# The modulation's products on VectorE instead of TensorE, in a two-block transformer kernel

## The chip, the cores and the metric

The kernel runs on one core of a Trainium2 chip. The metric is the device time of one execution in microseconds (us); the median of a few executions is quoted. A core has five engines with their own queues of instructions: PE (TensorE, matrix products), DVE (VectorE), ACT (ScalarE), POOL (GpSimd) and SP (SyncE, which here only starts DMA transfers). Each engine takes its instructions in order, and waits for the others through semaphores.

## What is computed

One batch of 256 tokens of 1024 features goes through two layers of a first block (three mixing branches, a gated feed-forward and a per-layer gate) and then through two layers of a second block, which also carries 256 context tokens. All tensors are float32. The second block modulates its normalized input by numbers that come from two vectors, `c` and `c_ctx`, through a matrix of 1024 x 6144 for each layer:

```
s_lat, s_ctx = silu(c), silu(c_ctx)[None, :]
for i in range(DEPTH):                                   # DEPTH = 2
    sh1, sc1, g1, sh2, sc2, g2 = split(s_lat @ ada_w[i] + ada_b[i], 6)
    a_l = rms_norm(h_lat, norm_g[i, 0]) * (1 + sc1) + sh1
    if ctx_in:                                           # both layers
        csh1, csc1, cg1, csh2, csc2, cg2 = split(s_ctx @ ada_w[i] + ada_b[i], 6)
        a_c = rms_norm(h_ctx, norm_g[i, 0]) * (1 + csc1) + csh1
    ...                                                  # pooling (i = 0) or attention (i = 1)
    h_lat = h_lat + g1 * y_l
    h_lat = h_lat + g2 * sq_relu_mlp(rms_norm(h_lat, norm_g[i, 1]) * (1 + sc2) + sh2)
    if ctx_out:                                          # only i = 0
        h_ctx = ...                                      # the same with the csh, csc and cg
```

So layer 0 needs all 6144 modulation numbers for both vectors, and layer 1 needs all of them for `c` but only the first 2048 (`csh1`, `csc1`) for `c_ctx`. These products are vector times matrix: 2 x 1024 x 6144 weights are read once each and used for at most two multiplications.

## The kernel before

**Tiling.** Activations lie with a feature to a partition: `x` is 128 partitions x 8 feature blocks x 256 tokens. Every weight is cut on the host into blocks of 128 x 128, and eight blocks make a chunk of 128 x 1024 (512 KB). `_plan` (L264) lists all 610 chunks in the order in which the program consumes them: 514 chunks of ordinary weights (`u`, `ug`, `kr`, ... `m211`) and 96 of the modulation's matrix (`ada0` and `ada1`, 48 each). The function `add` in it drops an ada chunk behind an ordinary one whenever the running sum `due` of the `share` arguments reaches 1, so `share=0.5` means one ada chunk behind every second ordinary chunk.

**The stream.** `Stream` (L310) loads ordinary chunks into four `raw` buffers by DMAs from SP, and ada chunks into two buffers of their own (`ADA_BUFS`). An ordinary chunk is then split in two float32r tiles: ACT rounds it to `hi` (L372), and DVE makes `lo = raw - hi` (L381). There are five `hi` and five `lo` buffers, so casts run at most four chunks ahead of the product in progress. `mm3` (L565) forms each product of a block by three matmuls, `hi` by the high part of the activation (L567), `hi` by its low part (L568) and `lo` by its high part (L569).

**The loop.** `linear` (L616) walks through the blocks of one weight. At each chunk's start it calls `st.get`, which writes the pending `lo` subtractions, the next casts and the next loads, and `bg_step`, which advances background work (norms, splits, softmax pieces, the context's pooling). Where a PSUM bank is complete it calls the evacuation. At each chunk's end `chunk_end` (L611) looks whether the plan has an ada chunk next, and if so calls `ada_chunk` (L592). The order in which the program is written is the order on every engine (`manual_schedule`, L434).

**The modulation before.** `ada_chunk` multiplies on PE: four matmuls (L602) of 128 rows x 256 columns, with `c` and `c_ctx` (after Silu, in the zero-padded tile `s32`) as two of 32 stationary columns, each into its own group of 32 partitions. Sixteen chunks, which are eight pieces of 256 features in two halves of the input, share one PSUM bank. Then ACT copies the bank out (L608), and `ada_turn` (L577) transposes it with two PE transposes (L584), sums the four groups on DVE (L587) and adds the bias `adab` (L590). There are six such turns. `mod_cols` (L1289) later makes `1 + scale` times the norm's gain. It runs for layer 0 inside the background work `ctx_pool` (L1396, during the second `ff`), and for layer 1 right behind `m101` (L1535).

**Names of the stages**, in the order of the plan: `u ug kr fq fk fv ga gc uq uk uv brc bra gb brb wo ff dn pl pg`, once for each layer of the first block (a digit 0 or 1 behind the name), the attentions running inside `ga` to `brb`; then `m100`, `m200`, `m101`, `m201` (the second block's first layer, the first two once for the context and once for `x`, `m101` on both at once), `k v q awo m110 m111 m210 m211`. In the kernel before, `ada0` is consumed from `ff0` to `fk1` and `ada1` from `ff1` to the second `m200`.

Of the kernel before, what the change touches and what calls it, by code (L numbers as in the profile page):

```python
# [30 lines left out]
AG = 8  # L31
# [64 lines left out]
def _weights(I):  # L96
# [6 lines left out]
    for i in range(DEPTH):  # L103
# [53 lines left out]
def _param_cols():  # L157
# [22 lines left out]
def _params(I):  # L180
# [238 lines left out]
def body(ctx: ExitStack, tc: tile.TileContext, dram, outT):  # L419
# [153 lines left out]
    s32 = cp.tile([P, 8, 2 * AG + 30], F32, name="s32")  # L573
    ada_r = cp.tile([P, 2, P], F32, name="ada_r")
    ada_at = {}

    def ada_turn():  # L577

        if "done" not in ada_at:
            return  # L580
        i, c = ada_at.pop("done")
        pt = sc_p.tile([P, 512], F32, tag="sc", name="pt_ada")
        for e in range(2):
            T.transpose(pt[:, e * P:(e + 1) * P], ada_r[:, e], ident)  # L584
        for e in range(2):
            o = ada[:, i, :, c + e:c + 2 * AG:2]
            V.reduce_sum(out=o.rearrange("p c q -> p q c"), axis=AX.X,  # L587
                         in_=pt[:, e * P:(e + 1) * P].rearrange("p (g q c) -> p q c g", g=4, c=2)[:, 0:AG])
        o = ada[:, i, :, c:c + 2 * AG]
        V.tensor_tensor(out=o, in0=o, in1=pc(f"adab{i}", c, c + 2 * AG)[:, None, :].to_broadcast([P, 2, 2 * AG]), op=ALU.add)  # L590

    def ada_chunk():  # L592

        name, c, _ = plan[st.pos]
# [2 lines left out]
        q, half = c // 2 % AG, c % 2
        if q == half == 0:
            ada_at["bank"] = sc_p.tile([P, 512], F32, tag="sc", name="ps_ada")
        ps = ada_at["bank"]  # L600
# [1241 lines left out]
```

## Time and profile before

| what | value |
| --- | --- |
| median of three executions | 1687.11 us (1686.91 to 1689.14) |
| the profiled execution | 1686.17 us, of which the span of the profile is 1684.4 us |
| PE busy | 1663.3 us (99%) |
| DVE busy | 1148.6 us (68%) |
| ACT busy | 889.4 us (53%) |
| POOL busy | 127.5 us (8%) |
| bytes moved | 329.76 MB, mean 196 GB/s |
| granted PE clock | mean 0.998 of full speed |

The span is the time between the first and the last instruction of the profile; 1.8 us of the execution lie around it, and the median stands 0.9 us above the profiled execution. PE's busy time counts overlapping matmuls once, so a PE at 99% says that it almost never waits, not that each product is at its fastest. Durations of DVE instructions include a short tail in which the next instruction may already run, so two neighbours can overlap by about 0.08 us.

### The profile page before, as it was taken

The numbers are of one execution on the slowest core, as the hardware profiler recorded it, in microseconds if no ns is written. First come the engines' busy times: TensorE is split into PE (matmuls) and PEld (weight loads), VectorE is DVE, ScalarE is ACT, GpSimd is POOL, SyncE is SP. The second block draws the span as 40 slices with busy tenths as digits, with TensorE's granted clock in tenths as the row PEclk, the third lists the DMA queues.
The fourth block names the chain that finished last, engine by engine and source line by source line (L and its number), as shares of the span: only waits on it lengthen the run. The fifth ranks groups of instructions, "written<-read, shape, count | busy, mean of one in ns | idle before, by whom it ended". The sixth has DMA issues, their size and how long they took to land.

```text
span 1684.4 us, 33981 instructions
## 1 busy us (share of the span) xinstructions
PE 1663.3 (99%) x14106; PEld 1582.2 (94%) x14106; DVE 1148.6 (68%) x1757; ACT 889.4 (53%) x1329; POOL 127.5 (8%) x128
## 2 busy tenths in 40 slices
PE   8999999999999999999999999999999999999998
PEld 7999998999989899999999999999999999899998
DVE  7888876564577788776886569664446666766654
ACT  6665564443455565655555455553334565667633
POOL 6100100000020000011000000100000011010001
PEclk9999999999999999999999999999999999999999
DMA  7546557777676465577767666666326554145553
GB/s 260 172 148 189 173 172 260 249 252 252 241 244 238 164 176 176 163 257 236 227 214 261 222 218 239 232 218 212 113 89 190 189 178 130 52 161 188 188 189 100
DMA packets 91738, 329.76 MB, mean 196 GB/s; under 512 B 10400, under 2 KB 11072, under 8 KB 91456
## 3 DMA queue, kind: packets, MB, share of 16 engines
q1 hardware_dynamic: 89712, 322.19, 57.6%
q10 hardware_dynamic: 1296, 4.33, 0.8%
q8 instruction: 110, 1.80, 0.4%
q0 software_dynamic: 576, 1.08, 0.3%
q14 instruction: 44, 0.36, 0.1%
HBM read 325.43 MB, written 1.05 MB: 194 GB/s over the span
## 4 chain that ended last, share of the span: by engine, by line
PE 92%; issue 3%; DVE 2%; POOL 1%; ACT 0%; DMA 0%; SPq 0%; POOLq 0%; DVEq 0%; ACTq 0%
PE ps_mm L567 27%; PE ps_mm L568 26%; PE ps_mm L569 26%; PE ps_ada L602 3%; PE sc L781 1%; PE ps_o L822 1%; POOL cols L714 1%; DVE lo L381 1%; PE ps_go L1693 1%; PE ps_w L1080 1%; PE ps_w L1081 1%; PE ps_w L1079 1%; PE ps_l L849 0%; PE sc L782 0%; PE ps_gt L1687 0%
## 5 line engine op out<-in xcount | busy, mean ns | idle before, releaser
L372 ACT ACTIVATE hi<-raw 128x1024 fp32r<-128x1024 f32 x513 | 537.8, 1057 | 386.2 <-PE ps_mm L568 291.4
L381 DVE TENSOR_TENSOR lo<-raw,hi 128x1024 fp32r<-128x1024 f32 x513 | 620.9, 1228 | 96.5 <-ACT hi L372 94.0
L567 PE MATMUL ps_mm<-S1h_t,hi 128*128 128x256 f32 (+1 forms) x1456 | 413.5, 284 | 0.0
L568 PE MATMUL ps_mm<-S1l_t,hi 128*128 128x256 f32 (+1 forms) x1456 | 405.7, 279 | 0.0
L569 PE MATMUL ps_mm<-S1h_t,lo 128*128 128x256 f32 (+1 forms) x1456 | 405.3, 278 | 0.0
L567 PE MATMUL ps_mm<-S0h_t,hi 128*128 128x256 f32 x1200 | 339.6, 283 | 6.3 <-ACT hi L362 6.3
L569 PE MATMUL ps_mm<-S0h_t,lo 128*128 128x256 f32 x1200 | 333.9, 278 | 0.2 <-DVE lo L381 0.2
L568 PE MATMUL ps_mm<-S0l_t,hi 128*128 128x256 f32 x1200 | 333.9, 278 | 0.1
L567 PEld LDWEIGHTS ps_mm<-S1h_t,hi 128*128 128x128 f32 x1456 | 274.5, 189 | 17.1 <-issue 15.5
L568 PEld LDWEIGHTS ps_mm<-S1l_t,hi 128*128 128x128 f32 x1456 | 274.1, 188 | 0.3
L569 PEld LDWEIGHTS ps_mm<-S1h_t,lo 128*128 128x128 f32 x1456 | 274.3, 188 | 0.0
L567 PEld LDWEIGHTS ps_mm<-S0h_t,hi 128*128 128x128 f32 x1200 | 226.9, 189 | 15.3 <-issue 7.3
L569 PEld LDWEIGHTS ps_mm<-S0h_t,lo 128*128 128x128 f32 x1200 | 226.2, 188 | 0.6 <-DVE lo L381 0.4
L568 PEld LDWEIGHTS ps_mm<-S0l_t,hi 128*128 128x128 f32 x1200 | 226.3, 189 | 0.4 <-DVE S0l_t L751 0.3
L692 POOL TENSOR_TENSOR acc<-acc,sq 128x512 f32<-128x512 f32 x24 | 34.4, 1435 | 817.8 <-ACT sq L684 817.7
L567 PE MATMUL ps_mm<-K_t,hi 128*128 128x256 f32 x320 | 89.6, 280 | 0.0
L568 PE MATMUL ps_mm<-GG_t,hi 128*128 128x256 f32 x320 | 88.5, 276 | 0.0
L569 PE MATMUL ps_mm<-K_t,lo 128*128 128x256 f32 x320 | 88.4, 276 | 0.0
L567 PE MATMUL ps_mm<-VV_t,hi 128*128 128x256 f32 x288 | 80.5, 279 | 0.0
L569 PE MATMUL ps_mm<-VV_t,lo 128*128 128x256 f32 x288 | 79.6, 276 | 0.0
L1493 DVE TENSOR_TENSOR P_t<-P_t 128x512 f32<-128x512 f32 x32 | 21.4, 690 | 77.5 <-ACT P_t L1492 77.5
L568 PE MATMUL ps_mm<-GX_t,hi 128*128 128x256 f32 x256 | 70.9, 277 | 0.0
(434 smaller groups left out, 3070.1 us busy)
## 6 DMA issues: line engine op xcount, KB each, us to landing
raw<-in_w_m_dram SPq DMA_DIRECT2D x176, 512.0 KB, 4.3
raw<-in_w_ada_dram SPq DMA_DIRECT2D x96, 512.0 KB, 4.4
raw<-in_w_ff_dram SPq DMA_DIRECT2D x88, 512.0 KB, 4.5
raw<-in_w_dn_dram SPq DMA_DIRECT2D x44, 512.0 KB, 4.6
raw<-in_w_ga_dram SPq DMA_DIRECT2D x16, 512.0 KB, 4.1
raw<-in_w_gc_dram SPq DMA_DIRECT2D x16, 512.0 KB, 3.6
raw<-in_w_gb_dram SPq DMA_DIRECT2D x16, 512.0 KB, 4.2
raw<-in_w_wo_dram SPq DMA_DIRECT2D x16, 512.0 KB, 3.6
```

The costliest lines, as they stand in the source:

```text
L372: self.nc.scalar.activation(out=h[:, :n], in_=raw[:, :n], func=AF.Copy)
L381: self.nc.vector.tensor_tensor(out=l[:, :n], in0=raw[:, :n], in1=h[:, :n].bitcast(F32), op=ALU.subtract)
L567: T.matmul(ps, lhsT=wh, rhs=ah, start=first, stop=False, skip_group_check=free)
L568: T.matmul(ps, lhsT=wh, rhs=al, start=False, stop=False, skip_group_check=free)
L569: T.matmul(ps, lhsT=wl, rhs=ah, start=False, stop=last, skip_group_check=free)
L602: T.matmul(ps[32 * g:32 * g + 32, 0:256], lhsT=s32[:, 4 * half + g, 2 * (AG - 1 - q):2 * (AG - 1 - q) + 32], rhs=w[:, g, :], start=(q == h ...
L692: e.tensor_tensor(out=self.acc[:, 0:n, :], in0=self.acc[:, 0:n, :], in1=sq[:, 0:n, :], op=ALU.add)
L714: G.tensor_tensor(out=self.cols, in0=v, in1=mhalf[:, 0:2], op=ALU.pow)
L781: T.matmul(sc[:, 0:256], lhsT=q[:, h, 128:256], rhs=k[:, h, :], start=True, stop=True)
L822: T.matmul(o[64 * e:64 * e + 64, 128 * kt:256], lhsT=self.v[:, kt, 64 * h:64 * h + 64], rhs=self.pT[e][:, 256 * kt:256 + 128 * kt], start= ...
L1079: T.matmul(banks[t], lhsT=a_h, rhs=wh[:, k % 2, :], start=(k == 0), stop=False)
L1493: V.tensor_tensor(out=r, in0=r, in1=r, op=ALU.mult)
```

## The change

The modulation's products leave PE. The host now lays `ada_w` out transposed, so that a chunk of 128 x 1024 holds 128 output features, one to a partition, with all 1024 inputs along the free dimension. `c` and `c_ctx` arrive copied to all 128 partitions (`cvec`, 128 x 2048, 1 MB, by a DMA on ACT's queue behind `ug0`), and ACT takes the Silu of both. `ada_chunk` is now one DVE instruction for each vector: multiply the chunk by the vector, write the products to `aprod`, and write their sum along the input to one column of `ada`. For `ada0` that is two instructions for each chunk, for `ada1` two in the first 16 chunks and one in the other 32: 48 x 2 + 16 x 2 + 32 = 160 instructions of 128 x 1024. The matmuls, the transposes, ACT's copies, the sums and the per-turn bias adds are gone; the bias is added in `mod_cols`, in four instructions. The ada chunks are also spread out more: fewer in `ff0`, `dn0`, `pg0` and in `u1` to `fk1`, some in `fv1` to `wo1`, fewer in `ff1` to `m200`, and 13 in `m101`.

```
-        a = I["ada_w_2"][i].reshape(2, 4, P, 24, 256)
-        W[f"ada{i}"] = a.transpose(2, 3, 0, 1, 4).reshape(P, -1)
+        W[f"ada{i}"] = I["ada_w_2"][i].T.reshape(48, P, D).transpose(1, 0, 2).reshape(P, -1)
...
         for n in ("u", "ug", "kr", "fq", "fk", "fv"):
-            add(f"{n}{i}", share=0.5 * i)
+            add(f"{n}{i}", share=0.4 * i)
         for n in ("ga", "gc", "uq", "uk", "uv", "brc", "bra", "gb", "brb", "wo"):
-            add(f"{n}{i}")
-        share = 0.5 - 0.15 * i
+            add(f"{n}{i}", share=0.17 * i)
+        share = 0.4 - 0.2 * i
...
-    add("m100", share=0.35)
+    add("m100", share=0.3)
...
-    for n in ("m101", "m201", "m201", "k", "v", "k"):
+    add("m101", share=0.9)
+    for n in ("m201", "m201", "k", "v", "k"):
...
-        A.activation(out=s32[:, :, 2 * AG - 2:2 * AG], in_=pc("c").rearrange("p (k c) -> p k c", c=2), func=AF.Silu)
+        for c in range(2):
+            A.activation(out=cvec[:, c], in_=cvec[:, c], func=AF.Silu)
...
-        w = st.get(name, c).rearrange("p (k n) -> p k n", k=4)
...
-        for g in range(4):
-            T.matmul(ps[32 * g:32 * g + 32, 0:256], lhsT=s32[:, 4 * half + g, 2 * (AG - 1 - q):2 * (AG - 1 - q) + 32],
-                     rhs=w[:, g, :], start=(q == half == 0), stop=(q == AG - 1 and half == 1),
-                     tile_position=(0, 32 * g), skip_group_check=True)
-        if q == 1 and half == 0:
-            ada_turn()
-        if q == AG - 1 and half == 1:
-            A.activation(out=ada_r, in_=ps[:, 0:256].rearrange("p (e x) -> p e x", e=2), func=AF.Copy)
-            ada_at["done"] = (i, c - 2 * AG + 1)
+        w = st.get(name, c)
+        for v in range(2 if i == 0 or c < 16 else 1):
+            V.scalar_tensor_tensor(out=aprod, in0=w, scalar=1.0, in1=cvec[:, v], op0=ALU.mult, op1=ALU.mult,
+                                   accum_out=ada[:, i, v, c:c + 1])
+        ada_done[i] += 1
...
+        if i == 0:
+            nc.scalar.dma_start(out=cvec, in_=dram["cvec"].rearrange("p (c k) -> p c k", c=2))
...
+        V.tensor_tensor(out=ada[:, i, c, 0:used], in0=ada[:, i, c, 0:used], in1=pc(f"adab{i}", 0, used), op=ALU.add)
```

On PE, at the border of two chunks in the middle of `ff0`, with the numbers of the buffers (`hi_3128` and its successor are two ordinary chunks), there stands before:

```order
L568 MATMUL ps_mm_3158<-S1l_t_2860,hi_3128 128x256
L569 MATMUL ps_mm_3158<-S1h_t_2859,lo_3129 128x256
L602 MATMUL ps_ada_3205<-raw_2080,s32_123 32x256 x4
L567 MATMUL ps_mm_3307<-S1h_t_2859,hi_3144 128x256
L568 MATMUL ps_mm_3307<-S1l_t_2860,hi_3144 128x256
L569 MATMUL ps_mm_3307<-S1h_t_2859,lo_3145 128x256
```

and in the changed kernel, at the same border (its lines 563 to 565 are `mm3`):

```order
L564 MATMUL ps_mm_3159<-S1l_t_2860,hi_3128 128x256
L565 MATMUL ps_mm_3159<-S1h_t_2859,lo_3129 128x256
L563 MATMUL ps_mm_3299<-S1h_t_2859,hi_3145 128x256
L564 MATMUL ps_mm_3299<-S1l_t_2860,hi_3145 128x256
L565 MATMUL ps_mm_3299<-S1h_t_2859,lo_3146 128x256
```

The four matmuls between the chunks are gone, here and at the other 95 places; nothing else on PE moved.

On DVE, in the same part of `ff0`, the kernel before alternates evacuations (`PP_t<-ps_mm,row` and the two behind it), casts (`lo<-raw,hi`) and the splits of the hidden values (`GX_t<-`):

```order
L1236 TENSOR_TENSOR PP_t<-ps_mm,row 128x512
L1239 TENSOR_TENSOR PP_t<-ps_mm,row 128x512
L1240 TENSOR_TENSOR PP_t<-PP_t 128x512
L381 TENSOR_TENSOR lo<-raw,hi 128x1024 x2
L751 TENSOR_TENSOR GX_t<-PP_t,Q_t 128x512
L1236 TENSOR_TENSOR PP_t<-ps_mm,row 128x512
L381 TENSOR_TENSOR lo<-raw,hi 128x1024 x2
L1239 TENSOR_TENSOR OA_t<-ps_mm,row 128x512
L1240 TENSOR_TENSOR OA_t<-OA_t 128x512
```

and the changed kernel (L377 is the cast, L1209 to L1213 the evacuation, L722 the split):

```order
L1209 TENSOR_TENSOR PP_t<-ps_mm,row 128x512
L1212 TENSOR_TENSOR PP_t<-ps_mm,row 128x512
L1213 TENSOR_TENSOR PP_t<-PP_t 128x512
L377 TENSOR_TENSOR lo<-raw,hi 128x1024
L578 SCALAR_TENSOR_TENSOR aprod,ada<-raw,cvec 128x1024 x2
L377 TENSOR_TENSOR lo<-raw,hi 128x1024
L722 TENSOR_TENSOR GX_t<-PP_t,Q_t 128x512
L1209 TENSOR_TENSOR PP_t<-ps_mm,row 128x512
L377 TENSOR_TENSOR lo<-raw,hi 128x1024 x2
L1212 TENSOR_TENSOR OA_t<-ps_mm,row 128x512
L1213 TENSOR_TENSOR OA_t<-OA_t 128x512
L578 SCALAR_TENSOR_TENSOR aprod,ada<-raw,cvec 128x1024 x2
```

A pair of products now stands between the casts, so the casts, evacuations and splits behind it on DVE come later by the pair's length.

On DVE in `ga1`, at the first softmax of the second layer (`smx` are the sums of the exponentials, `PP_t` the probabilities, which PE transposes next), before:

```order
L875 TENSOR_SCALAR GX_t<-VV_t 128x256
L1103 TENSOR_TENSOR PP_t<-ps_mm,row 128x512
L804 RECIPROCAL smx<-smx 128x2
L806 TENSOR_SCALAR PP_t<-PP_t,smx 128x256
L806 TENSOR_SCALAR PP_t<-PP_t,smx 128x128
```

and after:

```order
L846 TENSOR_SCALAR GX_t<-VV_t 128x256
L1076 TENSOR_TENSOR PP_t<-ps_mm,row 128x512
L578 SCALAR_TENSOR_TENSOR aprod,ada<-raw,cvec 128x1024 x2
L775 RECIPROCAL smx<-smx 128x2
L777 TENSOR_SCALAR PP_t<-PP_t,smx 128x256
L777 TENSOR_SCALAR PP_t<-PP_t,smx 128x128
```

A pair of products came in ahead of the normalization for which PE's transposes wait.

## Rows read from the trace of the kernel before

**Rows 1.** The page: busy time of PE and DVE, and the chain's shares by engine.

```profile
PE 1663.3 (99%) x14106; PEld 1582.2 (94%) x14106; DVE 1148.6 (68%) x1757; ACT 889.4 (53%) x1329; POOL 127.5 (8%) x128
...
PE 92%; issue 3%; DVE 2%; POOL 1%; ACT 0%; DMA 0%; SPq 0%; POOLq 0%; DVEq 0%; ACTq 0%
```

**Rows 2.** Waits of PE, longest first: who for whom, total us, times, longest.

```profile
PE ps_mm L567 <- ACT hi L362: 6.3, 1, 6.3
PE ps_r L719 <- POOL cols L714: 2.9, 7, 0.5
```

**Rows 3.** Timeline of PE around one ada chunk in `ff0`: start, us, instruction.

```profile
262.00 0.28 PE L567 MATMUL ps_mm<-S1h_t,hi 128*128 128x256 f32 x1
...
262.24 0.28 PE L569 MATMUL ps_mm<-S1h_t,lo 128*128 128x256 f32 x1
262.45 0.64 PE L602 MATMUL ps_ada<-raw,s 128*32 128x256 f32 x8
...
263.24 0.29 PE L568 MATMUL ps_mm<-S1l_t,hi 128*128 128x256 f32 x1
```

**Rows 4.** Instructions on the tile of the transposes: count, duration ns min/median/max, first and last.

```profile
L584 PE MATMUL pt_ada<-cst,ada_r x12: 271/272/328, 369.3 to 1265.0; 128*128 128x128 f32 x12
```

**Rows 5.** The page: DMA issues, count, KB each, median us to landing.

```profile
raw<-in_w_ada_dram SPq DMA_DIRECT2D x96, 512.0 KB, 4.4
```

**Rows 6.** DMAs by line: the transfer on ACT's queue nearest to `cvec`.

```profile
OC_t<-in_lruw_dram ACTq DMA_DIRECT2D x2, 512.0 KB, 5.4
```

**Rows 7.** Busy time by stage: start:end, us, PE, PEld, DVE, ACT, POOL, clock, DMA, GB/s.

```profile
249.03:388.31 139.28, 138.83 (x1242) 126.76 (x1241) 82.50 (x96) 61.72 (x72) 1.64 (x1) 1.00 0.75 246
388.31:457.02 68.71, 68.71 (x621) 62.79 (x617) 34.72 (x35) 28.14 (x34) 2.64 (x2) 1.00 0.72 253
457.02:551.20 94.18, 93.31 (x821) 84.92 (x817) 67.48 (x104) 53.31 (x79) 13.66 (x12) 1.00 0.70 241
551.20:648.39 97.19, 96.72 (x763) 90.70 (x759) 83.65 (x150) 57.31 (x106) 4.71 (x8) 1.00 0.54 163
648.39:737.12 88.73, 88.73 (x756) 86.65 (x754) 69.99 (x121) 49.13 (x93) 9.47 (x6) 1.00 0.55 181
737.12:877.38 140.26, 140.26 (x1248) 131.62 (x1247) 109.82 (x170) 74.29 (x99) 9.34 (x6) 1.00 0.74 245
877.38:978.66 101.28, 100.84 (x897) 94.69 (x895) 62.87 (x84) 50.47 (x69) 5.49 (x4) 1.00 0.65 224
978.66:1082.72 104.06, 104.06 (x927) 98.12 (x927) 85.26 (x133) 60.64 (x85) 6.77 (x5) 1.00 0.68 233
1082.72:1265.02 182.30, 182.30 (x1621) 176.91 (x1619) 87.52 (x102) 72.46 (x93) 0.00 (x0) 1.00 0.49 163
```

**Rows 8.** DVE and ACT instructions by line and form: count, busy us, mean ns, idle before.

```profile
L381 DVE TENSOR_TENSOR lo<-raw,hi 128x1024 fp32r<-128x1024 f32 x513 | 620.9, 1228 | 96.5 <-ACT hi L372 94.0 <-PE ps_mm L568 1.5
...
L1277 DVE SCALAR_TENSOR_TENSOR PP_t<-PP_t,Q_t 128x512 f32<-128x512 f32 x8 | 5.5, 683 | 0.0
...
L1756 DVE COPY hb<-ps_mm 128x1 f32<-128x1 f32 x32 | 4.9, 154 | 19.4 <-PE ps_mm L569 19.4
...
L886 DVE TENSOR_TENSOR_SCAN GX_t<-VV_t,S0h_t 128x256 f32<-128x256 f32 x4 | 2.7, 686 | 0.0
...
L796 ACT ACTIVATION_READ_ACCUMULATOR PP_t<-sc,mx 128x1 f32 x64 | 12.6, 196 | 0.0
```

**Rows 9.** Timeline of DVE in `ff0`: two casts back to back.

```profile
301.44 2.35 DVE L381 TENSOR_TENSOR lo<-raw,hi 128x1024 fp32r<-128x1024 f32 x2
```

**Rows 10.** The page: the costliest group of ACT, the casts, and what ended their waits.

```profile
L372 ACT ACTIVATE hi<-raw 128x1024 fp32r<-128x1024 f32 x513 | 537.8, 1057 | 386.2 <-PE ps_mm L568 291.4
```

**Rows 11.** Timeline in `ga1`: the first softmax's normalization on DVE, its transpose on PE.

```profile
585.78 0.55 DVE L806 TENSOR_SCALAR PP_t<-PP_t,smx 128x256 f32<-128x256 f32 x2
...
588.01 0.27 PE L812 MATMUL ps_t<-cst,PP_t 128*128 128x128 f32 x1
```

More of the change, by code (lines that the diff above doesn't have):

```diff
@@ L30 @@
 QA = 4
-AG = 8
 SW = S + 32
@@ L172, in _param_cols @@
     c.add("kg", 1)
-    c.add("c", 16)
     return c
@@ L208, in _params @@
     put("kg", _col(I["attn_k_g_2"][0]))
-    cc = np.stack([_col(I["c_2"][0]), _col(I["c_ctx_2"])], 2)
-    put("c", cc.reshape(P, 16))
     return out
@@ L292, in _plan @@
             add(f"{n}{i}", share=share)
-    add("m100", share=0.35)
-    add("m200", 0, LATA, 0.35)
+    add("m100", share=0.3)
+    add("m200", 0, LATA, 0.3)
     add("pool")
-    add("m200", LATA, None, 0.35)
-    add("m100", share=0.35)
-    add("m200", share=0.35)
-    for n in ("m101", "m201", "m201", "k", "v", "k"):
+    add("m200", LATA, None, 0.3)
+    add("m100", share=0.3)
+    add("m200", share=0.3)
+    add("m101", share=0.9)
+    for n in ("m201", "m201", "k", "v", "k"):
         add(n)
@@ L543, in prepare @@
         yield
-        G.memset(s32, 0.0)
     def prepare_ada():
-        A.activation(out=s32[:, :, 2 * AG - 2:2 * AG], in_=pc("c").rearrange("p (k c) -> p k c", c=2), func=AF.Silu)
+        for c in range(2):
+            A.activation(out=cvec[:, c], in_=cvec[:, c], func=AF.Silu)
     ada = cp.tile([P, 2, 2, 48], F32, name="ada")
@@ L569, in mm3 @@
         T.matmul(ps, lhsT=wl, rhs=ah, start=False, stop=last, skip_group_check=free)
[L573 to L590, printed above, removed]
+    cvec = cp.tile([P, 2, D], F32, name="cvec")
+    aprod = cp.tile([P, D], F32, name="aprod")
+    ada_done = [0, 0]
     def ada_chunk():
@@ L595, in ada_chunk @@
         i = int(name[3])
-        w = st.get(name, c).rearrange("p (k n) -> p k n", k=4)
[L597 to L600, printed above, removed]
-        for g in range(4):
-            T.matmul(ps[32 * g:32 * g + 32, 0:256], lhsT=s32[:, 4 * half + g, 2 * (AG - 1 - q):2 * (AG - 1 - q) + 32],
-                     rhs=w[:, g, :], start=(q == half == 0), stop=(q == AG - 1 and half == 1),
-                     tile_position=(0, 32 * g), skip_group_check=True)
-        if q == 1 and half == 0:
-            ada_turn()
-        if q == AG - 1 and half == 1:
-            A.activation(out=ada_r, in_=ps[:, 0:256].rearrange("p (e x) -> p e x", e=2), func=AF.Copy)
-            ada_at["done"] = (i, c - 2 * AG + 1)
+        w = st.get(name, c)
[3 more added lines that the diff above has]
+        ada_done[i] += 1
     def chunk_end():
@@ L1289, in mod_cols @@
     def mod_cols(i, c):
-        if ada_at.get("done", (None,))[0] == i:
-            ada_turn()
-        for n in range(2):
+        assert ada_done[i] == 48
+        used = 48 if i == 0 or c == 0 else 16
+        V.tensor_tensor(out=ada[:, i, c, 0:used], in0=ada[:, i, c, 0:used], in1=pc(f"adab{i}", 0, used), op=ALU.add)
+        for n in range(used // 24 if used == 48 else 1):
             sc = ada[:, i, c, 8 + 24 * n:16 + 24 * n]
@@ L1815 @@
     arrays = {}
-    nc = _bacc.Bacc("TRN2", target_bir_lowering=False, num_devices=1, dynamic_dma_scratch_size=8192)
+    nc = _bacc.Bacc("TRN2", target_bir_lowering=False, num_devices=1, dynamic_dma_scratch_size=4096)
     def given(name, a):
@@ L1832 @@
         "p": given("p", np.concatenate([_tokT(I["p"][i, 0]) for i in range(DEPTH)], 1)),
+        "cvec": given("cvec", np.broadcast_to(np.concatenate([I["c_2"][0], I["c_ctx_2"]])[None], (P, 2 * D))),
         "cst": given("cst", _consts()),
```

## The prediction

> **What bounds the kernel now.** I read the page's busy times first, then the chain, the waits of PE, and the busy time by stage. PE is busy for 99% of the span and DVE for 68%; the chain that ended last is 92% PE work [rows 1]. The list of PE's waits opens with 6.3 us at the start of the program, one wait, and 2.9 us over seven norms [rows 2]: hardly anything holds PE up. So each stage lasts as long as its PE work, and an instruction taken off PE is worth its full time, until another engine needs longer for that stage than PE does. DVE is the one to watch, because the change gives it the work. The reader should see in the table by stage [rows 7] how near DVE already is to PE: 82.5 of 139.3 us in `ff0` (the first row), but 83.7 of 97.2 from `fk1` to `uk1` (the fourth), 109.8 of 140.3 in `ff1` (the sixth) and 85.3 of 104.1 in the first `m100` and `m200` (the eighth). The fifth row is `brc1` to `wo1`, the second `dn0`, the third `pl0` to `fq1`, the seventh `dn1` to `pg1`, the ninth the second `m100` and `m200` and then `m101`. The granted clock is 1.00 in all of them.
>
> **What PE gets back.** Two neighbouring matmuls start 0.12 us apart (262.00 to 262.24 is two steps). Between the L569 at 262.24 and the L568 at 263.24 there are two such steps and the ada chunk [rows 3]. So one ada chunk costs PE 1.00 - 2 x 0.12 = 0.76 us, and there are 96 [rows 5]: 73.0 us. The 12 transposes of 0.27 us [rows 4] are pipelined; I count 1 us for them, between 0 and 3.3. Since PE is the chain, all 74 us lie on the path. If DVE never became late, the span would be 1684.4 - 74 = 1610.4 us.
>
> **What one product costs on DVE.** No row shows this instruction: a scalar_tensor_tensor over 1024 float32 elements with two sources in SBUF and a sum beside it. The nearest rows: the cast, a two-source instruction on the same 1024 elements, 1228 ns [rows 8], and two of them back to back in 2.35 us, 1.18 each [rows 9]; a scalar_tensor_tensor with two SBUF sources, 683 ns for 512 elements, so the kind as such is no slower [rows 8]. The sum has to be written out to one column. On ACT a separate instruction does that for 196 ns; a one-column instruction on DVE takes 154, part of which overlaps with its neighbour [rows 8]. So I take c = 1.18 + 0.12 = 1.30 us for each product, with 1.18 (the read-out free) and 1.42 (1.23 and ACT's 0.20) as the near ends. The far end is a DVE row that carries a value from element to element, as a running sum does: the scan, 686 ns for only 256 elements [rows 8]. From 512 and 1024 elements (683 and 1228 ns) the fixed part is 0.14 us and an element 1.06 ns; the scan's element is then (686 - 138) / 256 = 2.14 ns, and 1024 of them make 2.33 us. I stay with 1.30, because a sum that is only read at the end resembles the plain rows more than a scan whose every partial sum is written.
>
> [...]
>
> **The balance by stage.** PE's time of a stage without the change's matmuls is its length less 0.76 us for each ada chunk it now holds (22, 11, 14, 1, 0, 16, 11, 11, 10 in the nine rows). DVE's is its busy time plus c for each product that the new plan puts there (34, 18, 22, 14, 8, 18, 14, 9, 23; together 160) [rows 7]. With c = 1.30:
> `ff0` 122.6 on PE against 126.7 on DVE, DVE over by 4.1; `dn0` 60.3 against 58.1, 2.2 to spare; `pl0` to `fq1` 83.5 against 96.1, over by 12.5; `fk1` to `uk1` 96.4 against 101.9, over by 5.4; `brc1` to `wo1` 88.7 against 80.4, 8.3 to spare; `ff1` 128.1 against 133.2, over by 5.1; `dn1` to `pg1` 11.9 to spare; the first `m100` and `m200` 95.7 against 97.0, over by 1.3; the last row 57 to spare, `m101` with its 13 products included.
> The overruns add up to 28.5 us. With c = 1.18 they are 16.8, with 1.42 they are 40.1, with 2.33 they are 147.
> Not all of this reaches PE, since the casts run ahead. ACT's casts mostly wait for PE to release a buffer (291.4 us, the largest part of their idle time) [rows 10], so they stand as far ahead as the five buffers let them: four chunks of 24 matmuls, 4 x 24 x 0.12 = 11.5 us, less one chunk, because the subtraction is written one chunk after its cast, and less 1.06 + 1.23 us for the two: some 6 us, an estimate. A single pair of products (2.6 us) therefore hides completely. An overrun eats the lead first: 4.1 in `ff0` is hidden and half regained in `dn0`; the 17.9 us from `pl0` to `uk1` have 4.1 us of lead to eat and lose 13.8; `ff1` and what follows are hidden. That makes 13.8 us if the load within a stage were even. It is not (the context's pooling fills the middle of `ff1`, the scan chain the beginning of `ga1`), so I take the middle between this and 28.5: **21 us lost to DVE**.
>
> **The smaller terms.** *Softmax:* in `ga1` a pair now stands ahead of the first normalization. That ended at 585.78 + 0.55 = 586.33, and PE's transposes began at 588.01 [rows 11]: 1.7 us of cover against 2.6, so 0.9 us late, once; the other pairs in the attention stand elsewhere. I take 1 us, between 0 and 5. *`cvec`:* its 1 MB goes out on ACT's queue right ahead of `lruw`, whose 512 KB took 5.4 us to land [rows 6]; it can push back two chunks' loads while the lead is still small. 1 us, between 0 and 5. *ACT* takes two Silu of 1024 elements instead of one small one, about 2 x 1.06 us [rows 10], once, under the same lead. *SP:* its loads of ada chunks used to wait for PE's matmuls and now wait for DVE's products; the ordinary loads queued behind them wait for DVE's later subtractions anyway, and an ada chunk lands in 4.4 us [rows 5], two buffers ahead. Nothing. *DVE* loses the sums and adds of six turns and gains four bias adds: a few us less, counted at nothing. *POOL* loses one memset.
>
> **Sum.** 1684.4 - 73.0 - 1 + 21 + 1 + 1 = 1633.4 us of span. The profiled execution took 1.8 us more than its span, and the median of the runs 0.9 more than that execution: **1636 us**, 3.0% faster.
>
> **Rivals.**
> *DVE keeps up.* The read-out costs nothing, the lead covers every overrun, and all of PE's 74 us are kept: 1610.4 + 2.7 = 1613, up to 1621 with a small loss. For it: the load now moves out of the way in `m101`. Against it: from `pl0` to `uk1` even 1.18 us leaves DVE 13.6 us over. Chance 0.16.
> *The sum runs at half rate.* The accumulation takes two steps for each element, as the scan does: 2.33 us for a product, 147 us of overruns, 1610.4 + 147 + 2 + 2.7 = 1762, slower by 4.4%. This decides from about c = 1.72 us, where the overruns reach the 74 us that PE saves (18 in `ff0`, 5 in `dn0`, 22 up to `fq1`, 11 up to `uk1`, 13 in `ff1`, 5 in the first `m100` and `m200`). For it: the scan's row. Against it: the plain rows. Chance 0.14.
> *Late by order, not by load.* DVE takes its queue in order, so a pair also delays the evacuations and softmax steps behind it. If each of the 64 pairs made PE wait by what the softmax lacks, 0.9 us, that would be 58 us: 1613 + 58 = 1671. For it: the attentions, `ga1` above all, have no lead for the probabilities. Against it: in the linear stages four PSUM banks stand between PE and the evacuations. Chance 0.11.
>
> **How the numbers follow.** The forecast has 0.59, its own range is 1621 (c = 1.18 with the lead counted in full, 13.6 - 6 = 7.6 us lost, small terms nothing: 1610.4 + 7.6 + 2.7) to 1663 (c = 1.42, 40.1 us lost, small terms at 10). The range of 1612 to 1672 adds the first and the third rival and leaves out the second and tails, 0.18. About 0.2% is what a measurement of this kernel can tell from no change. Faster 0.83 (0.59, 0.16 and most of the third), same 0.03, slower 0.14.
>
> **What would show it.** No L602 and L584 on PE. A product of 1.2 to 1.3 us, with a small read-out behind it, confirms c; one over 1.7 us means the second rival. PE's busy share should fall from 99% to about 97.5%, and its waits, which now hold almost none for DVE, should show `lo`: in `pl0` to `uk1` foremost, with DVE busy for over 95% there, little in `ff0`, hardly any in `dn0`, `brc1` to `wo1` and from `m101` on. If PE waits evenly in all stages that hold products, the third rival is right. If the stages with DVE to spare do not shorten by 0.76 us for each ada chunk they held, the first term is wrong.

## The result: 1.1% faster, where 3.0% was forecast

The changed kernel took 1668.82 us (median of four runs, 1661.61 to 1675.58) against 1687.02 before. The ratio is 0.9889, 95% interval 0.984 to 0.9937. The profiled execution is the slowest of the four, 1675.58 us with a span of 1673.8. All changed kernels also have a DMA scratch size of 4096 instead of 8192, an edit that the section on the change does not list; what it does alone was not measured.

Two rows of the page answer [rows 1], the busy times and the chain:

```profile
PE 1622.0 (97%) x13326; PEld 1586.4 (95%) x13326; DVE 1326.3 (79%) x2062; ACT 886.7 (53%) x1324; POOL 127.0 (8%) x127
...
PE 75%; DVE 16%; issue 6%; POOL 2%; ACT 1%; DMA 0%; SPq 0%; DVEq 0%; POOLq 0%; ACTq 0%
```

PE executes 780 instructions fewer but is busy for only 41 us less, not 74, and DVE now holds 16% of the chain. The new instruction, from the view of its line (count, ns min/median/max, first and last start):

```profile
L578 DVE SCALAR_TENSOR_TENSOR aprod<-raw,cvec x160: 1201/1220/1229, 260.4 to 1245.1; 128x1024 f32<-128x1024 f32 x160
L578 DVE DVE_READ_ACCUMULATOR aprod<-raw,cvec x160: 76/82/92, 261.6 to 1246.2; 128x1 f32 x160
```

The two records of a product add up to 1.22 + 0.08 = 1.30 us, what the prediction took. So neither a dearer product nor the half-rate rival is the reason. The list of PE's waits, two of which mattered before [rows 2]:

```profile
PE ps_r L690 <- POOL cols L685: 7.1, 10, 1.8
PE ps_mm L563 <- ACT hi L358: 5.9, 1, 5.9
PE ps_mm L565 <- DVE lo L377: 5.2, 7, 1.2
PE ps_t L783 <- DVE smx L775: 4.0, 2, 2.2
PE ps_l L820 <- DVE Q_t L924: 3.3, 1, 3.3
PE ps_p L565 <- DVE lo L377: 2.4, 1, 2.4
```

The names after the arrow are the point: `lo`, which the balance by stage is about, is one among several. The others are links of a chain in which PE is fed once: the sums of a softmax (`smx`), a normalized query (`Q_t`), the `cols` of a norm, which POOL makes of what DVE hands it. The busy time by stage, columns as in [rows 7]; the nine stretches begin and end with the same stages as there:

```profile
251.68:377.37 125.69, 125.21 (x1064) 125.02 (x1063) 119.57 (x160) 61.68 (x72) 1.62 (x1) 1.00 0.75 249
377.37:439.56 62.19, 62.19 (x531) 62.19 (x529) 55.30 (x71) 27.73 (x32) 3.13 (x2) 1.00 0.79 269
439.56:542.95 103.39, 91.82 (x704) 89.17 (x703) 92.60 (x144) 53.27 (x78) 14.74 (x12) 0.90 0.63 207
542.95:644.38 101.43, 96.83 (x752) 90.35 (x751) 97.22 (x175) 57.07 (x105) 4.71 (x8) 1.00 0.58 186
644.38:737.26 92.88, 89.85 (x755) 87.16 (x754) 81.22 (x139) 49.09 (x93) 9.76 (x6) 0.98 0.58 192
737.26:874.23 136.97, 130.53 (x1119) 129.40 (x1118) 129.76 (x204) 72.19 (x97) 8.23 (x6) 1.00 0.68 224
874.23:970.88 96.65, 94.40 (x806) 94.00 (x805) 78.81 (x108) 51.22 (x70) 6.12 (x5) 1.00 0.65 212
970.88:1072.67 101.79, 98.73 (x837) 97.60 (x836) 94.21 (x148) 60.06 (x84) 6.78 (x5) 1.00 0.68 226
1072.67:1253.58 180.91, 180.91 (x1539) 180.91 (x1538) 113.59 (x148) 71.99 (x92) 0.00 (x0) 1.00 0.60 203
```

Three things are to be seen, and each became a theory.

**DVE late.** The third row (`pl0` to `fq1`) takes 103.39 us, longer than it did with its 14 ada chunks on PE (94.18).

**The clock.** The third row's granted clock is 0.90. Inside `u1` it is 0.50 for 17 us, behind a stretch in which PE stood still for a quarter of the time (6.09 of 8.13 us busy):

```profile
468.67:476.80 8.13, 6.09 (x52) 5.70 (x50) 8.06 (x13) 3.02 (x5) 1.92 (x1) 1.00 0.51 170
476.80:493.80 17.00, 12.84 (x57) 12.25 (x58) 12.68 (x20) 8.16 (x11) 6.04 (x6) 0.50 0.56 184
```

**PE's pace.** In the second and the last row PE is busy without a gap at a granted clock of 1.00, and still longer than its work was priced: 62.19 us for 531 instructions, 117 ns for each. In the trace, neighbouring matmuls start either 113.3 or 117.8 ns apart, and one pace holds for long rows (117.8 ns from 263 to 454 us, 1627 instructions). Before, some 7 in 10 of the steps were at 113.3.

### The profile page after: what moved, and what is told of

Its sections match the earlier page's. It is cut to its first block, busy times and chain, and to the rows that moved or that the text cites. A ratio compares the mean times of both kernels' runs of the same rounds, so it can differ in the third digit from the quotient of the medians.

```text
span 1673.8 us, 32732 instructions
## 1 busy us (share of the span) xinstructions
PE 1622.0 (97%) x13326; PEld 1586.4 (95%) x13326; DVE 1326.3 (79%) x2062; ACT 886.7 (53%) x1324; POOL 127.0 (8%) x127
## 4 chain that ended last, share of the span: by engine, by line
PE 75%; DVE 16%; issue 6%; POOL 2%; ACT 1%; DMA 0%; SPq 0%; DVEq 0%; POOLq 0%; ACTq 0%
PE ps_mm L563 22%; PE ps_mm L564 22%; PE ps_mm L565 22%; DVE lo L377 6%; DVE aprod L578 2%; POOL cols L685 1%; PE sc L752 1%; PE ps_go L1667 1%; PE ps_o L793 1%; PE ps_gt L1661 0%; PE ps_l L820 0%; ACT hi L368 0%; POOL acc L663 0%; DMA x<-in_x_dram 0%; PE ps_r L690 0%
## 5 line engine op out<-in xcount | busy, mean ns | idle before, releaser
L377 DVE TENSOR_TENSOR lo<-raw,hi 128x1024 fp32r<-128x1024 f32 x513 | 623.4, 1233 | 57.2 <-ACT hi L368 56.4
L565 PE MATMUL ps_mm<-S1h_t,lo 128*128 128x256 f32 (+1 forms) x1456 | 410.9, 282 | 2.9 <-DVE S0h_t L962 1.7
L564 PE MATMUL ps_mm<-S1l_t,hi 128*128 128x256 f32 (+1 forms) x1456 | 410.9, 282 | 1.2 <-DVE S1l_t L711 1.2
L564 PEld LDWEIGHTS ps_mm<-S1l_t,hi 128*128 128x128 f32 x1456 | 278.6, 191 | 1.8 <-DVE S1l_t L711 1.4
L563 PEld LDWEIGHTS ps_mm<-S1h_t,hi 128*128 128x128 f32 x1456 | 278.6, 191 | 1.1 <-issue 0.7
L578 DVE SCALAR_TENSOR_TENSOR aprod<-raw,cvec 128x1024 f32<-128x1024 f32 x160 | 195.3, 1220 | 2.2
```

Source lines behind the costliest of these rows:

```text
L377: self.nc.vector.tensor_tensor(out=l[:, :n], in0=raw[:, :n], in1=h[:, :n].bitcast(F32), op=ALU.subtract)
L563: T.matmul(ps, lhsT=wh, rhs=ah, start=first, stop=False, skip_group_check=free)
L564: T.matmul(ps, lhsT=wh, rhs=al, start=False, stop=False, skip_group_check=free)
L565: T.matmul(ps, lhsT=wl, rhs=ah, start=False, stop=last, skip_group_check=free)
L578: V.scalar_tensor_tensor(out=aprod, in0=w, scalar=1.0, in1=cvec[:, v], op0=ALU.mult, op1=ALU.mult, accum_out=ada[:, i, v, c:c + 1])
```

## Experiments

In the tables and the text a stage's length runs from its first matmul to the first of the next stage. "Short products" keeps every instruction, wait and transfer, but each product reads 2 elements.

### The same kernel once more

> The changed kernel itself, profiled a second time. The gain of 74 us that PE was to bring came to 18, and its trace shows three places for the difference: the granted clock at half for 24 us behind PE's waits (about 12 us lost), matmuls that follow each other at 117.8 ns instead of 113.3 in long rows (about 20 us), and waits for DVE (about 20 us). If the slow rows and the halved clock are settled by the program, the same stages show them again and the time is 1669 within 3 us. If they are settled by the moment, where a row happens to start, other stages are slow, and the time lies anywhere between 1660 and 1676.

Measured: 1663.15 us (1661.66 to 1667.84), ratio 0.9866 (0.985 to 0.9882); profiled span 1662.7, 11.1 us less than the first. Two windows inside `ff0` and `dn0`, the first profile and then the second:

```profile
260.00:360.00 100.00, 99.52 (x845) 99.33 (x846) 96.79 (x129) 47.15 (x54) 1.62 (x1) 1.00 0.77 257
380.00:430.00 50.00, 50.00 (x427) 50.00 (x426) 44.88 (x58) 22.85 (x27) 2.62 (x2) 1.00 0.79 268
```

```profile
260.00:360.00 100.00, 99.52 (x877) 99.32 (x877) 98.08 (x131) 47.34 (x55) 1.63 (x1) 1.00 0.78 259
380.00:430.00 50.00, 50.00 (x444) 50.00 (x443) 48.08 (x62) 24.02 (x29) 3.07 (x2) 1.00 0.82 286
```

With the same busy time at the same clock PE executes 877 instructions in one and 845 in the other: one program, two paces. `ff0` took 121.4 us here and 125.7 there, `dn0` 59.8 and 62.2. So the pace is not settled by the program alone, and it makes some 9 of the 11 us between these two profiles (the other executions have no profile). The halved clock in `u1` came back (13.7 us at 0.50 here, 17 in the first, `u1` 24.2 us in both): that one stands in both profiles of the program.

### Short products, everywhere and in the middle

```
+        n = 2
...
-            V.scalar_tensor_tensor(out=aprod, in0=w, scalar=1.0, in1=cvec[:, v], op0=ALU.mult, op1=ALU.mult,
+            V.scalar_tensor_tensor(out=aprod[:, 0:n], in0=w[:, 0:n], scalar=1.0, in1=cvec[:, v, 0:n], op0=ALU.mult, op1=ALU.mult,
```

> Each product reads 2 elements instead of 1024, so the modulation's sums are left out but for two terms; every instruction, wait and transfer stays. DVE gets back some 180 us. If all of the missing gain is DVE being late, the time is PE's floor, 1610 to 1616. If PE's pace is a loss of its own, that has nothing to do with how busy DVE is, the waits and the halved clock go (32 us) and the slow rows stay: 1630 to 1645, with ff0 and dn0 still at about 117.8 ns a matmul. If a busy DVE is what slows the matmuls, ff0 goes to 113 to 114 ns.

> Only the products between the first and the second feed-forward layer (pl0 to wo1), which is where PE waited and the clock fell, read 2 elements instead of 1024; the modulation's sums are left out there but for two terms. If DVE's lateness there made the waits and the halved clock, both go in these stages: u1 24.2 to 12 to 13, fq1 21.5 to 15, bra1 18.2 to 14, ga1 29.7 to 27.5, in all 22 to 30 us, so 1640 to 1648. If the halved clock comes from something else (a weight's arrival, the order on PE), these stages keep it and no more than 10 us are gained.

Measured: everywhere 1624.82 us (1620.45 to 1625.75), ratio 0.9629 (0.9615 to 0.9643); in the middle alone 1642.17 (1635.75 to 1654.07), ratio 0.976 (0.9718 to 0.9803). The first time lies between the two ranges expected. The second lies in its first range, though `u1` with 15.9 us, instead of 12 to 13, does not. By stage, in us; the first two columns are the prediction's own balance (PE's without the ada matmuls, DVE's with c = 1.30):

| stretch | PE, predicted | DVE, predicted | changed, 1st | changed, 2nd | short in the middle | short everywhere |
|---|---|---|---|---|---|---|
| up to `ff0` | 249.0 | | 251.7 | 251.3 | 251.4 | 249.8 |
| `ff0` | 122.6 | 126.7 | 125.7 | 121.4 | 121.4 | 120.7 |
| `dn0` | 60.3 | 58.1 | 62.2 | 59.8 | 59.8 | 59.8 |
| `pl0`-`fq1` | 83.5 | 96.1 | 103.4 | 102.9 | 86.7 | 86.7 |
| `fk1`-`uk1` | 96.4 | 101.9 | 101.4 | 101.5 | 96.3 | 96.3 |
| `brc1`-`wo1` | 88.7 | 80.4 | 92.9 | 91.1 | 88.7 | 88.7 |
| `ff1` | 128.1 | 133.2 | 137.0 | 138.0 | 137.2 | 131.1 |
| `dn1`-`pg1` | 92.9 | 81.0 | 96.7 | 94.2 | 96.7 | 94.8 |
| 1st `m100`, `m200` | 95.7 | 97.0 | 101.8 | 101.8 | 101.6 | 97.4 |
| 2nd, and `m101` | 174.7 | 117.4 | 180.9 | 180.9 | 174.1 | 174.1 |
| rest | 419.4 | | 420.2 | 419.7 | 420.0 | 419.3 |

With short products the span is 1618.7 us, 8 more than PE's predicted floor of 1610.4, and 44 less than in the second profile. (By the medians the two kernels differ by 38 us; the profile with short products is the fastest execution of its four.) Of the 44, 35.8 lie in the six stretches from `ff0` to the first `m200` in which PE waits (0.7 + 16.2 + 5.2 + 2.4 + 6.9 + 4.4), 24 of them between `pl0` and `wo1`, and there all of it goes with the middle products alone. Single rows can be off by 1 to 2 us, because the paces differ too: `wo1`, at PE's full busy time in both, takes 21.8 us in the second profile and 22.6 with short products. The 6.8 us of the last but one row are pace, not waiting, as the rows of that stretch show (second profile of the changed kernel, then short products):

```profile
1062.10:1243.01 180.91, 180.91 (x1539) 180.91 (x1538) 113.61 (x148) 72.03 (x92) 0.00 (x0) 1.00 0.60 204
```

```profile
1025.34:1199.41 174.07, 174.07 (x1538) 174.07 (x1537) 89.46 (x149) 72.03 (x93) 0.00 (x0) 1.00 0.61 211
```

The run with short products in the middle has full ones in this stretch and takes 174.1 us, as long as with short ones: the full products on DVE did not slow the matmuls there.

### What halves the clock in `u1`

Even with short products `u1` is 3.5 us longer than PE's work there (15.85 against 13.84 - 2 x 0.76 = 12.3). PE waits once, for 2.3 us, and right behind that the clock is 0.50 for 3.4 us:

```profile
PE ps_n L674 <- DVE acc L668: 2.3, 1, 2.3
```

```profile
469.80:473.20 3.40, 3.40 (x17) 3.17 (x17) 3.10 (x4) 1.15 (x2) 2.43 (x2) 0.50 0.76 207
```

```
             ps = ms_p.tile([P, 512], F32, tag="ms", name="ps_n")
+            if st.plan[st.pos - 1][0] == "u1":
+                fill = sc_p.tile([P, 512], F32, tag="sc", name="ps_fill")
+                for _ in range(5):
+                    T.matmul(fill[:, 0:256], lhsT=ident, rhs=cst[:, 0:256], start=True, stop=True)
             self.sums(ps)
```

> The kernel with short products (sums left out but for two terms), and in u1, right ahead of the row sums for which PE stands still 2.6 us there, five matmuls of an unused result (about 2.2 us). [...] If PE's standing still brings the halved clock, it goes with the filled hole, and u1 takes 14.0 to 14.4 us. If it has another cause, the halved stretch stays and u1 takes 15.8 us or more.

Measured in one execution: 1623.10 us. In the window around `u1` the granted clock is now 1.00 throughout:

```profile
458.00:475.00 17.00, 15.76 (x128) 14.95 (x127) 15.08 (x29) 10.34 (x15) 4.28 (x4) 1.00 0.62 197
```

So the halved stretch went with PE's standing still for those 2.3 us, in one execution. But `u1` fell only to 15.5 us, not to 14.0 to 14.4. The fill stands where the wait was, and PE now waits 1.1 us at the next link of the same norm, where without the fill, with the clock at 0.50, the list of waits has none:

```profile
PE ps_r L695 <- POOL cols L690: 1.1, 1, 1.1
```

So the 3.4 us at 0.50 cost little of their own here (15.85 against 15.5 us). Before the change an ada chunk stood 3 us ahead of this norm's sums, and PE did not wait for them:

```profile
495.40 0.64 PE L602 MATMUL ps_ada<-raw,s 128*32 128x256 f32 x8
...
498.48 0.50 PE L702 MATMUL ps_n<-ones,acc 128*128 128x1 f32 x4
```

### Breaking the row of matmuls

```
         ada_done[i] += 1
+        if c % 16 == 0:
+            tick["bank"] = sc_p.tile([P, 512], F32, tag="sc", name="ps_tick")
+        T.matmul(tick["bank"][0:32, 0:2], lhsT=ident[:, 0:32], rhs=ident[:, 0:2], start=True, stop=True, skip_group_check=True)
```

> One matmul of two columns is put on PE at each place where a chunk of the modulation's weight is multiplied on DVE (96 of them, result unused), to break the row of the layers' matmuls where the old kernel's 4 matmuls broke it. If the pace of 113.3 or 117.8 ns is taken up anew at each break and held until the next, the stages with breaks mix both paces as before (some 7 rows in 10 at 113.3) and the time falls by 8 to 18 us, to 1651 to 1661. If the pace comes from the new places of the tiles in memory or from DVE's traffic, ff0 and dn0 stay at 117.8 and the time is the same or longer by the 96 matmuls, 1669 to 1680.

Measured: 1727.86 us, ratio 1.0243 (1.0228 to 1.0258), slower by far, and as an experiment half spoilt. The unused result held one of the two PSUM banks of the softmax, for which PE now waited:

```profile
PE sc L756 <- ACT PP_t L771: 33.2, 8, 5.7
```

Where no softmax runs, `m101` and the latent `m100` and `m200` had 113.3 ns throughout, where both profiles without ticks had 117.8; but other kernels below had 113.3 there without a tick. A tick itself cost 0.33 us in `ff0` ((127.0 - 121.4) / 17). Counted over the whole profile, some 8 in 10 of the steps at either pace are at 113.3 ns with ticks, against 7 in 10 before the change and 3 and some 5 in 10 in the two profiles of the changed kernel. That fits the idea that a break takes up the pace anew, but a kernel without ticks below (new places with split pair) has 7 in 10 too, so it is not shown. At its price breaking rows is no cure, and what draws the pace stays open.

### Burst, load or place

Why is DVE late? The timeline of DVE in the second profile, on the way into `u1`, shows one case (start, us, instruction):

```profile
463.55 0.69 DVE L1251 TENSOR_TENSOR x<-x,PP_t 128x512 f32<-128x512 f32 x1
464.16 1.22 DVE L578 SCALAR_TENSOR_TENSOR aprod<-raw,cvec 128x1024 f32<-128x1024 f32 x1
465.31 0.08 DVE L578 DVE_READ_ACCUMULATOR aprod<-raw,cvec 128x1 f32 x1
465.42 1.22 DVE L578 SCALAR_TENSOR_TENSOR aprod<-raw,cvec 128x1024 f32<-128x1024 f32 x1
466.57 0.08 DVE L578 DVE_READ_ACCUMULATOR aprod<-raw,cvec 128x1 f32 x1
466.57 1.88 DVE L711 SCALAR_TENSOR_TENSOR S1l_t<-x,par,S1h_t 128x256 fp32r<-128x256 f32 x2
```

```profile
468.11 0.38 PE L564 MATMUL ps_mm<-S1l_t,hi 128*128 128x256 f32 x1 [1.24 <-DVE S1l_t L711]
```

A pair of products lies between the update of `x` and the split of it (L711), and PE, which needs the low half `S1l`, starts 1.24 us late. The lead of the casts is no help here: the late thing is an activation. In the first of two tests of the pair's length, its second product was issued half a chunk later:

```
+        product(0)
+        if i == 0 or c < 16:
+            second.append(lambda: product(1))
...
+            if b % CB == CB // 2:
+                later()
```

> The places of the changed kernel, but of each chunk's two products only the first stands behind the chunk; the second is issued half a chunk later, so that a waiting link has at most one product of 1.3 us ahead of it, not two. If the length of the burst (2.6 us) makes the waits, those of fq1, ga1, bra1 and the pool's (3.7, 2.5, 2.1, 2.7 us) lose up to 1.3 us each and one or two of the halved stretches go: 1650 to 1660. If it is the sum of work ahead of the link that counts, nothing moves: 1661 to 1672.

Measured: 1666.64 us, ratio 0.9887 (0.9863 to 0.9911): the total did not move (`ga1` lost 1.7 us, `gc1` gained 0.6), so the length of the burst is not what decides. Then seven chunks near such links were made whole in the kernel with short products, and, the mirror image, short in the changed kernel:

```
+LINKS = [("pg0", 6), ("u1", 1), ("u1", 3), ("kr1", 5), ("fq1", 2), ("fv1", 1), ("brc1", 2)]
...
+        n = D if at in LINKS else 2
```

> The kernel with short products (the modulation's sums left out but for a few terms), in which 7 of the 96 chunks get their products whole again, 14 products or 18 us of DVE: those behind the last chunks of pg0, kr1, fq1 and fv1, the two in u1 and the one in brc1, all of them shortly ahead of a place where the changed kernel's PE waited for DVE. If a product costs PE by what stands behind it in DVE's queue, these 7 bring back most of the 28 us between the run with short products in the middle and the changed kernel: 1640 to 1652, u1 at 20 us or more, fq1 at 17 or more, ga1 and bra1 at 1.5 us more. If the sum of DVE's work in a stage is what counts, 18 us more in 200 us with room for them cost next to nothing: 1622 to 1632.

> The mirror image of the run with 7 whole chunks: the changed kernel, in which just those 7 chunks (behind the last chunks of pg0, kr1, fq1, fv1, the two in u1, one in brc1) read 2 elements, so that their sums are left out, and the other 89 are whole. In the short kernel the 7 cost 11.7 us, 6.2 of it in u1. If each product has a price of its own that goes by its place, taking the 7 out of the changed kernel gives 10 to 14 us back: 1652 to 1657. If waits come from a backlog, where the last product of several decides, leaving out a third of the work in that stretch takes it below the point and more comes back than they cost alone, 18 to 26 us: 1640 to 1649, with ga1, bra1 and brb1 at 27.2, 14.0 and 11.4 us.

Measured: 1630.80 us (1629.14 to 1632.12) and 1656.43 us (1653.38 to 1663.2). The seven cost 8.6 us from `pl0` to `fq1` in the first (95.3 against 86.7) and give 10.3 back there in the second (92.6 against 102.9); `u1` moves by 6.2 and by 6.3 us. In the total the first run lies where the load theory put it, but `u1` lies where the link theory did: 22.0 us, while `fq1` grew by 1.4 only and `ga1` and `bra1` not at all, against my list of links. So I had one of the places right and several wrong. The two runs do agree that a product's price goes by its place: three pairs at `u1` cost 6 us, either way, partly as halved clock (10.2 us at 0.50 in the first of the two); up to `uk1` the other four cost 2.6 us alone and 5.2 among the rest, so what has piled up ahead of them seems to count too. (From `brc1` to `wo1` the second run was 1.8 us slower than the second profile. It has a halved stretch of 3.4 us there, as the first profile has.)

### Other places for the same products

`_plan` got a table of places instead of shares. First 34 chunks in `ff0` and `dn0` and none at the links seen so far; the same with the pair split; then, with the SiLU of the vectors moved ahead of `gc0`, the old density in `ff0` and `dn0` and 8 chunks in `gc0`, `gb0` and `wo0`; last, a few moved once more.

```
+    "ff0": [c for c in range(44) if c % 2 or c in (20, 30)], "dn0": [0, 2, 4, 6, 8, 11, 13, 15, 17, 19], "pl0": [1], "pg0": [2],
+    "ug1": [1, 3], "kr1": [0, 2, 4], "gc1": [1, 4], "gb1": [1, 4], "wo1": [1, 3, 5],
```

> The products stay whole and on DVE, only their places change: 34 of the first 48 chunks in ff0 and dn0, 12 in chunks where the second trace of the changed kernel showed no wait (ug1, kr1, gc1, gb1, wo1), none in u1, fq1, fk1, ga1, brc1, bra1, 6 of the second 48 in ff1's quiet middle and 20 in m101. If what is lost to DVE is lost at a few places where a product stands ahead of a link that PE is about to wait for (row sums, softmax, norms), the loss falls to a few us above the run with short products: 1626 to 1640. If it is DVE's load as such, ff0, dn0 and m101 now wait for lo halves and the time stays at 1645 to 1668.

> Both edits: the new places and the two products of a chunk half a chunk apart. If places alone settle it, the time is that of the run with new places within 4 us; if the burst still costs something there, 4 to 8 us less. If load is the cause, neither helps: 1645 or more.

> As the run with new places, but with ff0 and dn0 at the changed kernel's own density (17 and 9 chunks, where it showed no wait), the SiLU of the two vectors ahead of gc0 instead of ff0, so that 8 chunks can stand in gc0, gb0 and wo0, one chunk in kr1 instead of three, and none in m200c nor at the end of m100c; m101 takes 22. If a product costs only where it stands ahead of a link or where DVE is already full, ff0 comes back to 121 to 126 us, fq1 to 15 to 17, m200c to 51 to 53, and the time is 1625 to 1640. If moving them merely moves the wait, gc0, gb0 and wo0 each grow by 2 us or more and the time stays near 1650.

> As the run with earlier places (1637 us), with no product at the end of gc0 and gc1, none in kr1 and none in pg0 behind chunk 1; they stand in gb0, wo0, ff0 and gb1 instead. If these were the links there, u1 falls from 19.2 to 15.9 to 17 us and uq0 and uq1 from 11.2 and 10.2 to 9.4, and the time is 1628 to 1634. If u1 waits for something else than the products in pg0, it stays at 19 and the time at 1635 to 1638.

| kernel | us | ratio (95%) | `ff0` | `u1` | `fq1` | `fk1`-`uk1` | `brc1`-`wo1` | 1st `m200` |
|---|---|---|---|---|---|---|---|---|
| changed, 2nd | 1663.15 | 0.9866 (0.985 to 0.9882) | 121.4 | 24.2 | 21.5 | 101.5 | 91.1 | 55.4 |
| new places | 1655.41 | 0.9807 (0.9777 to 0.9837) | 132.5 | 16.9 | 20.6 | 96.7 | 88.7 | 57.0 |
| with split pair | 1650.70 | 0.9789 (0.9762 to 0.9815) | 129.1 | 16.6 | 20.4 | 96.3 | 88.7 | 56.3 |
| earlier places | 1637.44 | 0.9705 (0.9681 to 0.9728) | 125.8 | 19.2 | 15.8 | 97.2 | 88.7 | 54.1 |
| moved once more | 1639.59 | 0.9714 (0.9688 to 0.974) | 126.6 | 14.3 | 14.6 | 96.6 | 88.7 | 54.1 |

The new places missed the expected 1626 to 1640 and lie in the range for load: `u1` came back to 1.1 us above its length with short products and all from `fk1` to `wo1` to PE's own, but `fq1` stayed at 20.6 us, and `ff0` with 24 chunks instead of 17 filled up. Its window and its first wait (the stretch, then who waited for whom):

```profile
252.50:385.00 132.50, 126.89 (x1065) 124.54 (x1064) 129.98 (x179) 59.64 (x69) 1.63 (x1) 0.99 0.77 253
```

```profile
PE ps_mm L574 <- DVE lo L386: 4.6, 5, 1.8
```

There load does decide: DVE is busy for 98% (129.98 of 132.50 us) and PE waits 4.6 us for `lo`, while with 116.7 of 121.4 us, 96%, in the second profile the stretch was 0.7 us longer than with short products. The two runs with and without the split pair overlap in their intervals, which shows no gain. The earlier places gave 1637.44 us, the same 160 products as the changed kernel at 26 us less, and beat both kernels. (The first `m200`, 54.1 us, missed its 51 to 53.) In its list of waits from `ff0` to the start of `ff1`, the two longest, `lo`, `smx` and `Q_t` have all but gone:

```profile
PE ps_n L683 <- DVE acc L677: 2.7, 1, 2.7
PE ps_mm L575 <- DVE S0h_t L972: 1.3, 1, 1.3
```

The last version did free `u1` (14.3 us, no halved clock), and yet its time missed both ranges. Its executions lie between 1630.26 and 1643.84 us, so it does not differ from the earlier places by more than the noise. There is now a wait of 1.9 us for the norm at the start of `ff0`, and behind it 6.8 us at a granted clock of 0.50. The chunk that I added at the end of `wo0` is the likely cause; that was not tried alone.

```profile
PE ps_n L683 <- DVE acc L677: 1.9, 1, 1.9
```

```profile
265.60:272.40 6.80, 6.02 (x30) 5.83 (x29) 6.26 (x10) 4.68 (x6) 0.92 (x1) 0.50 0.78 243
```

## Where the prediction failed, and what held

The sign and the order of the terms held: faster, with DVE's lateness as the largest loss, foremost from `pl0` to `uk1`. The time lay inside the range, above the forecast's own; the gain was little more than a third of the forecast one.

- **The 21 us lost to DVE: the step that failed.** The prediction took the stages in which DVE has more work than PE, 28.5 us, let the casts' lead hide up to half, and chose the middle. The lead lets PE go on while `lo` is late. But in the first profile `lo` makes only 7.6 of some 26 us that PE waited for DVE. The others were mostly `smx`, `Q_t`, `acc` and halves of activations such as `S1l`, which have no lead, and behind them came 7.1 us for `cols`. The runs show 35.8 us instead of 21 and 1 for the softmax, which moves the sum by 14; 24 of them lie between `pl0` and `wo1`, and other places for the same products bring back 26 us of the time.
- **c = 1.30 us: right as a duration, 0.1 too high as a load.** The two records overlap with what follows: a pair holds DVE for 2.41 us (464.16 to 466.57 above), 1.20 for each product, and DVE's busy time rose by 177.7 us, 1.11 for each, net of what the turns took off it. With 1.20 the predicted overruns come to 18.8 us, not 28.5. The half rate of the second rival, 2.33 us after the scan's row, did not show: the product took 1.22 us for 1024 elements, where the plain cast took 1.23 [rows 8].
- **The balance by stage: near in size, in part by luck.** It gave 101.9 us for `fk1` to `uk1`, measured 101.5, and 133.2 for `ff1`, measured 138.0; its overruns sum to 28.5 us, the measured loss to 35.8. But DVE's busy time came out 2 to 7 us below the forecast in eight of the nine rows of the first profile (97.2 us in `fk1` to `uk1`), so PE waited where DVE was not full, and `brc1` to `wo1` lost 2.4 us where the balance had 8.3 to spare. The largest difference is the third stretch, 102.9 against 96.1. It has the halved clock, 17.1 us of it in the second profile against 3.4 with short products; at half the clock the 13.7 us more are worth at most 7 us, an estimate.
- **What PE gets back, 74 us, all on the path: nearly right as work, wrong as time.** With short products the span is 1618.7, so 66 of the 74 us arrive in that profile, and 62 by the medians. About 3.5 are missing in `u1`, where the ada chunks had filled a hole; most of the rest of the profile's 8 is pace, 113.3 against 117.8 ns. The announced test (0.76 us for each chunk in stages with DVE to spare) came out both ways: `dn0` gave back 8.9 us for its 11 chunks in the second profile and 6.5 in the first, where 8.4 were due, and the last of the nine rows 1.4 of 7.6 in both.
- **Left out altogether:** the granted clock, which was 1.00 in [rows 7] and which I took as given, and the pace. Beside the part of it that the run with short products has too, the pace is worth 6.8 us in the second profile (the stretch that ends with `m101`) and some 16 in the first (there, in `ff0`, `dn0` and `dn1` to `pg1`).

In the second profile: 1633.4 forecast + 14 (DVE, with the clock) + 7 (short products above the floor and `cvec`) + 8 (pace, and 1 us at the start) = 1662.4 against a span of 1662.7.

The rival "late by order" had the mechanism half right, and at 1671 the nearest time, but not in its form: an even 0.9 us for each pair. At `u1` three pairs cost 2 us each, while `ff0` with 17 pairs lost 0.7 us in all. "DVE keeps up" fell. The small terms, `cvec` and softmax, stayed within their bounds: the kernel reached `ff0` 2.3 to 2.7 us later, 0.6 to 1.6 of them already at the start of `kr0`, about when the transfer of `cvec` began, and PE's waits for `smx` sum to 4.0 us, but in two places, `ga1` and `bra1`, where one was forecast.

## What to carry to other kernels

Work that moves to an engine with idle time was nearly free here only where that engine was not full and nothing stood behind it on its queue that the busy engine takes next (17 pairs in `ff0` with DVE busy for 96%: 0.7 us; three pairs in `u1`: 6 us): price it at the links (norms, softmax, splits of activations), not by the share of busy time alone, and give no credit for a lead that belongs to other data. Filler work on the bounding engine may be covering waits: without the ada chunks PE waited 2.3 us in `u1` even with short products, with 3.4 us at a clock of 0.50 behind it, and taking the filler out gave back 62 to 66 of its 74 us. Once such a change is made, its places are worth more than its price: the same 160 products cost 38 us in one plan and 13 in another (1663 and 1637 against 1625 with short products).

## What the runs showed of the hardware

Not expected: rows of the same matmuls, at a granted clock of 1.00, ran at 113.3 or at 117.8 ns apiece, differed so between two executions of one program, and kept the pace for up to some 1960 instructions (in the first profile, from the second `m100` to the first half of `m201`, 1072.67 to 1303.40 us): 4%, some 9 of the 11 us between two profiles here. Behind one wait of PE of 2.3 us (short products) came 3.4 us at a granted clock of 0.50 in `u1`; with two waits of 1.2 and 1.7 us there it was 0.50 for 17 us from 476.8 us on, behind the first of them (first profile), and for 13.7 us from 471.8 us on, behind both (second). With the 2.3 us filled by useless matmuls the clock stayed at 1.00, in one execution. A wait alone does not settle it: behind 2.2 us for `smx` in `ga1` the clock stayed at 1.00 in both profiles, and behind the same 1.8 us in `bra1` it was halved for 3.4 us in the first and not in the second. What makes a halved stretch 3.4 us long or 17, and what draws the pace at its start, wasn't settled.
